# DeltaNet keys and head outputs: scaling by norms moved from GpSimd steps to one VectorE product with broadcast norms

## The chip, the cores and the metric

The kernel runs on one core of one Trainium2 chip. The time is device microseconds (us) of one execution, the median over runs. A profile is one further execution recorded by the hardware profiler. TensorE is called PE in the rows, its weight loads PEld, VectorE is DVE, ScalarE is ACT, GpSimd is POOL and the queue that issues most transfers is SP.

## The reference, cut to what matters

A two-layer encoder trunk over 1024 tokens of width 1024: layer 0 mixes tokens by attention, layer 1 by a bidirectional gated DeltaNet, and each is followed by a convolutional MLP. The change is in the DeltaNet mixer. The lines that it computes are these:

```
def l2norm(x):
    return x * lax.rsqrt(jnp.sum(x * x, axis=-1, keepdims=True) + EPS)
...
    q = jnp.repeat(l2norm(q.reshape(B, S, GDN_QK_HEADS, GDN_DK)) * (GDN_DK ** -0.5), rep, axis=2)
    k = jnp.repeat(l2norm(k.reshape(B, S, GDN_QK_HEADS, GDN_DK)), rep, axis=2)
...
    o = rmsnorm(o_fwd + o_bwd, o_norm) * jax.nn.silu(z ...)
```

There are 8 key heads of 128 numbers and 16 value heads of 128. Each key row of a token and each output row of a token is multiplied by one number, the inverse root of its sum of squares.

## The kernel before, in words

**Layout.** The mixer goes over eight key heads j, each with two value heads. For every j, `gdn_in` projects keys, queries, gates and values (TensorE, `dense`, line 134), runs the width-5 convolution (`conv5`, the VectorE steps on line 448) and prepares what the recurrence needs. `decay` and `inverse` build the inverse triangular matrices of the 128-token chunks, `chain` runs the recurrence over eight chunks in each direction, and `head_out` normalises, gates and stores the two heads.

**Keys.** Behind `kq` in `gdn_in`, the keys lie transposed, so four TensorE transposes (line 533) and a ScalarE copy (473) bring each half of 512 tokens into a tile `h` with tokens on the partitions: four blocks of 128 columns, one block for each 128 tokens. ScalarE sums the squares of each block (484). `rstd` takes the inverse root: a VectorE step (152) and a power on GpSimd (153). Then GpSimd multiplies each of the eight blocks by its column of `r` (line 496, tile `h` out of `h` and `rs`). For each half the result is stored by `put` (a transfer on SP's queue, 468), transposed back by four TensorE transposes (533) and copied to `kT` by ScalarE (499). `kT` feeds the products of line 515.

**Outputs.** In `head_out`, for each half, ScalarE sums squares (756), VectorE corrects them by the query norms (759), `rstd` runs again (152, 153), VectorE multiplies by the query norm (761), and GpSimd scales eight blocks of 128 columns (763, tile `o`). For each value head e, four TensorE transposes (770) read every other block, and VectorE applies the gate (771).

**What sets the order.** The program is written out without loops on the chip. Each instruction gets a priority from a counter that runs in program order; `ahead` lowers the counter for the instructions in it, so that they go before others. `gdn_in`'s key and query block stands in `ahead(2, 1100)`, `decay` and `inverse` in `ahead(4)`, `chain` in `ahead(2)`, and `head_out` has no such mark. When the program is built, a list scheduler lays each engine's instructions into one fixed queue from these priorities, the data they need, and the durations that it assumes. On the chip each queue runs strictly in that order: an instruction that waits holds up everything behind it on its engine. SP's queue, which issues the loads and stores, works the same way.

**Others on the same engines.** GpSimd also scales keys and state in `chain` (705 and 708, tiles `kd` and `sd`), and clears tiles in `inverse` (603, 604). VectorE runs the chain's steps (716, 722, 738, 744), the decay (553, 560, 561, 564), the inverse (608, 609, 624, 628), the weights' low halves (110) and the convolution (448).

Of the kernel before, what the change touches and what calls it, by code (L numbers as in the profile page):

```python
# [13 lines left out]
ALU = mybir.AluOpType  # L14
# [4 lines left out]
P = 128  # L19
# [22 lines left out]
class Trunk:  # L42
# [409 lines left out]
    def gdn_in(self, j, ys, tmp, dp, begun=None):  # L452


        nc = self.nc
        w, cw = self.ap["gdn_in"], self.cw5
        pk = self.dram.tile([NC, P, 5, P], F32, name=f"pk{j}")
        self.pk.append(pk)

        def proj(i):  # L460
            acc = self.big()
            self.dense(acc, self.weights(w[i]), ys)
            return acc

        chunks = lambda t: t.rearrange("p (n c) -> p n c", c=P)

        def put(i, t, ns=slice(0, NC)):
            nc.sync.dma_start(out=pk[ns, :, i].rearrange("n p c -> p n c"), in_=chunks(t))

        def natural(t, i):  # L470
            for h, hs in enumerate(HALVES):
                r = tmp.tile([P, H2], F32, name="h", bufs=2)
                nc.scalar.copy(out=r, in_=self.transposed(t[:, hs]))
                put(i, r, slice(4 * h, 4 * h + 4))

        kq = [self.conv5(acc, cw[:, c], tmp) for acc, c in zip(begun or (proj(8 + j), proj(j)), (8 + j, j))]
        with self.ahead(2, 1100):
            kT, qT = kq
            ss = [dp.tile([P, NC], F32, name="ssn", bufs=2) for _ in range(2)]

            def sums(t, tot):
                for n in range(4):
                    sq = dp.tile([P, P], F32, name="sq", bufs=1)
                    nc.scalar.activation(out=sq, in_=t[:, n * P:(n + 1) * P], func=AF.Square, accum_out=tot[:, n:n + 1])

            kn = []
            for h, hs in enumerate(HALVES):
                t = tmp.tile([P, H2], F32, name="h", bufs=2)
                nc.scalar.copy(out=t, in_=self.transposed(kT[:, hs]))
                sums(t, ss[0][:, 4 * h:4 * h + 4])  # L490
                kn.append(t)
            r = self.rstd(ss[0], 1, dp)
            for h, hs in enumerate(HALVES):
                for n in range(4):
                    t = kn[h][:, n * P:(n + 1) * P]
                    nc.gpsimd.tensor_scalar(out=t, in0=t, scalar1=r[:, 4 * h + n:4 * h + n + 1], scalar2=1.0,
                                            op0=ALU.mult, op1=ALU.mult)
                put(2, kn[h], slice(4 * h, 4 * h + 4))
                nc.scalar.copy(out=kT[:, hs], in_=self.transposed(kn[h]))
            for h, hs in enumerate(HALVES):  # L500
                sums(self.transposed(qT[:, hs]), ss[1][:, 4 * h:4 * h + 4])
            r = self.rstd(ss[1], 1, dp)
            self.rq.append(dp.tile([P, NC, 2], F32, name="rq", bufs=2))
            nc.vector.tensor_scalar(out=self.rq[j], in0=r.unsqueeze(2).broadcast_to([P, NC, 2]),
                                    scalar1=float(P) ** -0.5, scalar2=None, op0=ALU.mult)
            put(0, kT)
            put(1, qT)
            kks, qks = {}, {}
            for i in (1, 0):
                kks[i], qks[i] = (dp.tile([P, H2], F32, name=n, bufs=3) for n in ("kks", "qks"))  # L510
                for rhs, dst in ((kT, kks[i]), (qT, qks[i])):
                    acc = self.bank()
                    for n in range(4):
                        tok = slice((4 * i + n) * P, (4 * i + n + 1) * P)
                        nc.tensor.matmul(acc[:, n * P:(n + 1) * P], lhsT=kT[:, tok], rhs=rhs[:, tok], start=True, stop=True)
                    if rhs is kT:
                        nc.vector.tensor_tensor(out=chunks(dst), in0=chunks(acc), op=ALU.mult,
                                                in1=self.negoff.unsqueeze(1).broadcast_to([P, 4, P]))
                    else:
                        nc.scalar.copy(out=dst, in_=acc)  # L520
        z = lambda e: self.gate_rows(2 * j + e, proj(32 + 2 * j + e), tmp)
        z(0)
        z(1)
        for e in range(2):
            i = 16 + 2 * j + e
            natural(self.conv5(proj(i), cw[:, i], tmp), 3 + e)
        return kks, qks
# [218 lines left out]
    def head_out(self, j, o, dp):  # L746

        nc = self.nc
        od = [self.dram.tile([P, S], F32, name=f"od{2 * j + e}") for e in range(2)]
        for i in (1, 0):  # L750
            hs = HALVES[i]
            ss = dp.tile([P, 8], F32, name="ss", bufs=1)
            of = o[i].rearrange("p n e c -> p (n e) c")
            for m in range(8):
                sq = dp.tile([P, P], F32, name="sq", bufs=1)
                nc.scalar.activation(out=sq, in_=of[:, m], func=AF.Square, accum_out=ss[:, m:m + 1])
            rq = self.rq[j][:, 4 * i:4 * i + 4].rearrange("p n e -> p (n e)")
            for _ in range(2):
                nc.vector.tensor_tensor(out=ss, in0=ss, in1=rq, op=ALU.mult)
            rs = self.rstd(ss, P, dp, tag="ro")  # L760
            nc.vector.tensor_tensor(out=rs, in0=rs, in1=rq, op=ALU.mult)
            for m in range(8):
                nc.gpsimd.tensor_scalar(out=of[:, m], in0=of[:, m], scalar1=rs[:, m:m + 1], scalar2=1.0,
                                        op0=ALU.mult, op1=ALU.mult)
            for e in range(2):
                z = dp.tile([P, H2], F32, name="z", bufs=1)
                nc.sync.dma_start(out=z, in_=self.zd[2 * j + e][:, hs])
                pt = self.bank()
                for n in range(4):
                    nc.tensor.transpose(out=pt[:, n * P:(n + 1) * P], in_=o[i][:, n, e], identity=self.ident)  # L770
                nc.vector.scalar_tensor_tensor(out=z, in0=pt, scalar=self.o_gain, in1=z, op0=ALU.mult, op1=ALU.mult)
                nc.sync.dma_start(out=od[e][:, hs], in_=z)
        self.od += od
# [622 lines left out]
```

## Time and profile before

| What | us |
|---|---|
| median of 3 runs | 3466.25 |
| lowest and highest run | 3457.93, 3467.89 |
| the profiled execution's own time | 3468.96 |
| its span, first to last instruction | 3467.2 |
| DeltaNet stretch looked at, 1368 to 2610 us of the span | 1242 |

The mean granted TensorE clock of the profiled execution is 0.976 of full speed. In the rows further down, "idle before" is the time in which an engine did nothing before an instruction, and the name behind the arrow is the instruction that ended it.

### The profile page before, as it was taken

The numbers are of one execution on the slowest core, as the hardware profiler recorded it, in microseconds if no ns is written. First come the engines' busy times: TensorE is split into PE (matmuls) and PEld (weight loads), VectorE is DVE, ScalarE is ACT, GpSimd is POOL, SyncE is SP. The second block draws the span as 40 slices with busy tenths as digits, with TensorE's granted clock in tenths as the row PEclk, the third lists the DMA queues.
The fourth block names the chain that finished last, engine by engine and source line by source line (L and its number), as shares of the span: only waits on it lengthen the run. The fifth ranks groups of instructions, "written<-read, shape, count | busy, mean of one in ns | idle before, by whom it ended". The sixth has DMA issues, their size and how long they took to land. (4 is left out here: it accounts for less than half of the span.)

```text
span 3467.2 us, 54360 instructions
## 1 busy us (share of the span) xinstructions
PE 3266.1 (94%) x19690; PEld 2627.5 (76%) x19690; DVE 2474.7 (71%) x4203; ACT 1730.5 (50%) x3218; POOL 922.6 (27%) x1111
## 2 busy tenths in 40 slices
PE   7999999899999998899999999999898989999998
PEld 6887878677777776777777777777676867777776
DVE  5325886877776865877768687776853787777695
ACT  4235664544444454466655564555532544544452
POOL 1111220444442001133232223223230144444100
PEclk9999999999999999899999999999999989999999
DMA  4331116333335533233342433324256633332743
GB/s 126 107 113 55 33 33 203 111 110 112 98 101 189 197 116 100 70 112 108 92 145 70 132 109 108 114 82 137 82 190 197 199 103 110 107 99 96 240 132 108
DMA packets 249806, 411.23 MB, mean 119 GB/s; under 512 B 25537, under 2 KB 76097, under 8 KB 249537
## 3 DMA queue, kind: packets, MB, share of 16 engines
q1 hardware_dynamic: 249536, 407.76, 37.7%
q8 instruction: 155, 2.54, 0.3%
q14 instruction: 115, 0.93, 0.1%
HBM read 294.80 MB, written 107.61 MB: 116 GB/s over the span
## 5 line engine op out<-in xcount | busy, mean ns | idle before, releaser
L134 PE MATMUL mm<-base,wh 128*128 128x512 f32 x1248 | 484.0, 415 | 6.5 <-DVE t L448 6.4
L109 ACT CAST wh<-w_raw 128x512 fp32r<-128x512 f32 x275 | 170.1, 619 | 313.9 <-PE mm L134 181.7
L110 DVE TENSOR_TENSOR wl<-w_raw,wh 128x512 fp32r<-128x512 f32 x275 | 195.1, 713 | 150.9 <-ACT wh L109 140.4
L134 PE MATMUL mm<-yh,wh 128*128 128x512 f32 x736 | 286.0, 417 | 5.3 <-ACT t L291 2.7
L134 PE MATMUL mm<-yl,wh 128*128 128x512 f32 x736 | 282.1, 412 | 1.6 <-POOL yl L110 1.0
L153 POOL TENSOR_TENSOR rs<-rs,power 128x8 f32<-128x8 f32 (+2 forms) x38 | 63.4, 1669 | 822.0 <-DVE rs L152 821.7
L134 PE MATMUL mm<-yh,wl 128*128 128x512 f32 x736 | 280.1, 409 | 1.0 <-DVE wl L110 1.0
L134 PEld LDWEIGHTS mm<-base,wh 128*128 128x128 f32 x1248 | 240.4, 193 | 45.8 <-issue 4.2
L134 PE MATMUL mm<-base,wl 128*128 128x512 f32 x624 | 256.9, 412 | 6.2 <-DVE wl L110 6.2
L705 POOL TENSOR_SCALAR kd<-c,yds 128x128 f32<-128x128 f32 x224 | 92.5, 425 | 563.8 <-PE cp L734 373.7
L109 ACT CAST wh<-a 128x512 fp32r<-128x512 f32 x164 | 101.8, 621 | 252.7 <-PE mm L134 115.3
L134 PE MATMUL sp<-base,wh 128*128 128x512 f32 (+1 forms) x672 | 211.5, 373 | 12.4 <-ACT wh L109 12.4
L109 ACT CAST wh<-s 128x512 fp32r<-128x512 f32 x212 | 131.3, 619 | 176.3 <-PE sp L134 98.2
L448 DVE SCALAR_TENSOR_TENSOR t<-mm,gdn_cw,t 128x1023 f32<-128x1023 f32 (+1 forms) x128 | 163.0, 1275 | 8.3 <-ACT t L445 7.4
L134 PEld LDWEIGHTS mm<-yl,wh 128*128 128x128 f32 x736 | 140.9, 192 | 29.0 <-POOL yl L110 2.9
L134 PEld LDWEIGHTS mm<-yh,wh 128*128 128x128 f32 x736 | 140.5, 193 | 29.5 <-ACT t L291 3.6
L134 PEld LDWEIGHTS mm<-yh,wl 128*128 128x128 f32 x736 | 140.9, 192 | 25.5 <-DVE wl L110 1.7
L134 PE MATMUL sp<-base,wl 128*128 128x512 f32 (+1 forms) x432 | 157.6, 365 | 1.4 <-DVE wl L110 0.9
L134 PEld LDWEIGHTS sp<-base,wh 128*128 128x128 f32 x672 | 127.7, 190 | 34.0 <-ACT wh L109 12.8
L110 DVE TENSOR_TENSOR wl<-s,wh 128x512 fp32r<-128x512 f32 x170 | 141.8, 835 | 13.5 <-ACT wh L109 12.9
L982 POOL TENSOR_TENSOR s<-a,a 128x512 f32<-128x512 f32 x80 | 108.4, 1355 | 159.8 <-DVE s L982 106.7
L134 PEld LDWEIGHTS mm<-base,wl 128*128 128x128 f32 x624 | 119.5, 192 | 27.3 <-DVE wl L110 7.1
(522 smaller groups left out, 9417.8 us busy)
## 6 DMA issues: line engine op xcount, KB each, us to landing
a<-in_ffn_up_dram SPq DMA_DIRECT2D x160, 256.0 KB, 3.0
c<-pk SPq DMA_DIRECT2D x128, 320.0 KB, 3.1
w_raw<-in_gdn_in_dram SPq DMA_DIRECT2D x100, 256.0 KB, 2.9
g_t<-t SPq DMA_DIRECT2D x88, 256.0 KB, 2.0
raw<-g_t SPq DMA_DIRECT2D x88, 256.0 KB, 2.7
w_raw<-in_gdn_out_dram SPq DMA_DIRECT2D x68, 256.0 KB, 3.7
g<-t SPq DMA_DIRECT2D x66, 256.0 KB, 2.1
raw<-g SPq DMA_DIRECT2D x66, 256.0 KB, 2.9
```

The costliest lines, as they stand in the source:

```text
L109: self.nc.scalar.copy(out=hi, in_=src)
L110: (engine or self.nc.vector).tensor_tensor(out=lo, in0=src, in1=hi.bitcast(F32), op=ALU.subtract)
L134: self.nc.tensor.matmul(acc if one else acc[:, hs], lhsT=a, rhs=y[:, hs], start=(first and not onto and k + t == 0), stop=(last and k == n ...
L153: nc.gpsimd.tensor_tensor(out=r, in0=v, in1=self.power[:, :w], op=ALU.pow)
L448: nc.vector.scalar_tensor_tensor(out=o, in0=a, scalar=c[:, i:i + 1], in1=o, op0=ALU.mult, op1=ALU.add)
L705: nc.gpsimd.tensor_scalar(out=kd[:, e], in0=kn, scalar1=col(self.yds, e), scalar2=1.0, op0=ALU.mult, op1=ALU.mult)
L982: e.tensor_tensor(out=s[i], in0=x, in1=z, op=op)
```

## The change

The eight GpSimd steps on the keys become two VectorE products, one for each half, each over 128 partitions by 512 columns; the eight GpSimd steps for each half of the outputs become one VectorE product over 1024 columns. The norms enter as a second input that is broadcast along the 128 columns of a block. Nothing else is touched.

```diff
             r = self.rstd(ss[0], 1, dp)
             for h, hs in enumerate(HALVES):
-                for n in range(4):
-                    t = kn[h][:, n * P:(n + 1) * P]
-                    nc.gpsimd.tensor_scalar(out=t, in0=t, scalar1=r[:, 4 * h + n:4 * h + n + 1], scalar2=1.0,
-                                            op0=ALU.mult, op1=ALU.mult)
+                nc.vector.tensor_tensor(out=chunks(kn[h]), in0=chunks(kn[h]), op=ALU.mult,
+                                        in1=r[:, 4 * h:4 * h + 4].unsqueeze(2).broadcast_to([P, 4, P]))
                 put(2, kn[h], slice(4 * h, 4 * h + 4))
                 nc.scalar.copy(out=kT[:, hs], in_=self.transposed(kn[h]))
...
             rs = self.rstd(ss, P, dp, tag="ro")
             nc.vector.tensor_tensor(out=rs, in0=rs, in1=rq, op=ALU.mult)
-            for m in range(8):
-                nc.gpsimd.tensor_scalar(out=of[:, m], in0=of[:, m], scalar1=rs[:, m:m + 1], scalar2=1.0,
-                                        op0=ALU.mult, op1=ALU.mult)
+            nc.vector.tensor_tensor(out=of, in0=of, in1=rs.unsqueeze(2).broadcast_to([P, 8, P]), op=ALU.mult)
             for e in range(2):
```

## Rows read from the trace of the kernel before

**Rows 1.** The page: busy time, share of the span, instructions of each engine.

```profile
PE 3266.1 (94%) x19690; PEld 2627.5 (76%) x19690; DVE 2474.7 (71%) x4203; ACT 1730.5 (50%) x3218; POOL 922.6 (27%) x1111
```

**Rows 2.** Busy time by stretch: the DeltaNet stretch; columns as in the first line.

```profile
core 0: us, PE busy (x) PEld busy (x) DVE busy (x) ACT busy (x) POOL busy (x), PEclk, DMA share, GB/s
1368.00:2610.00 1242.00, 1157.17 (x9881) 911.26 (x9882) 919.66 (x2081) 686.37 (x1525) 337.13 (x685) 0.97 0.38 112
```

**Rows 3.** Groups by shape, GpSimd, that stretch: busy us, mean ns, idle before, releasers.

```profile
L763 POOL TENSOR_SCALAR o<-o,ro 128x128 f32<-128x128 f32 x128 | 60.6, 492 | 9.6 <-DVE ro L761 9.6
...
L153 POOL TENSOR_TENSOR rs<-rs,power 128x8 f32<-128x8 f32 x16 | 26.4, 1647 | 65.6 <-DVE rs L152 65.4
L496 POOL TENSOR_SCALAR h<-h,rs 128x128 f32<-128x128 f32 x64 | 23.1, 381 | 0.8
```

**Rows 4.** Line 496: who waited for it, us in total and times.

```profile
  PEld sp L533: 21.6, 31
...
  DVE st L738: 8.5, 3
```

**Rows 5.** Timeline of one key block: start, us, engine, line, idle before.

```profile
1941.87 1.64 POOL L153 TENSOR_TENSOR rs<-rs,power 128x8 f32<-128x8 f32 x1
...
1943.61 2.80 POOL L496 TENSOR_SCALAR h<-h,rs 128x128 f32<-128x128 f32 x8
1944.04 0.14 PEld L533 LDWEIGHTS sp<-ident,h 128*128 128x128 f32 x1 [2.37 <-POOL h L496]
...
1945.08 0.14 PEld L533 LDWEIGHTS sp<-ident,h 128*128 128x128 f32 x1 [0.21 <-POOL h L496]
...
1946.14 0.46 PEld L533 LDWEIGHTS sp<-ident,h 128*128 128x128 f32 x4
```

**Rows 6.** Line 763: who waited for it, us in total and times.

```profile
  PEld sp L770: 7.7, 8
```

**Rows 7.** Timeline of the last head's two halves of outputs.

```profile
2579.34 0.14 PEld L770 LDWEIGHTS sp<-ident,o 128*128 128x128 f32 x1 [2.52 <-POOL o L763]
...
2600.48 0.17 DVE L761 TENSOR_TENSOR ro<-ro,rq 128x8 f32<-128x8 f32 x1 [1.76 <-POOL ro L153]
2600.82 2.80 POOL L763 TENSOR_SCALAR o<-o,ro 128x128 f32<-128x128 f32 x8 [0.37 <-DVE ro L761]
2601.24 0.14 PEld L770 LDWEIGHTS sp<-ident,o 128*128 128x128 f32 x1 [2.57 <-POOL o L763]
...
2603.32 0.18 PEld L770 LDWEIGHTS sp<-ident,o 128*128 128x128 f32 x1 [0.30 <-POOL o L763]
```

**Rows 8.** Groups by shape, VectorE: products of two tensors.

```profile
L560 DVE TENSOR_TENSOR at<-pr,kks 128x512 f32<-128x512 f32 x64 | 44.4, 694 | 0.9 <-ACT pr L555 0.2
...
L517 DVE TENSOR_TENSOR kks<-sp,negoff 128x512 f32<-128x512 f32 x16 | 11.0, 686 | 6.8 <-PE sp L515 6.8
...
L1039 DVE TENSOR_TENSOR t<-t,t 128x1024 f32<-128x1024 f32 x44 | 53.6, 1219 | 0.0
```

**Rows 9.** Waits of VectorE in the DeltaNet stretch: us in total, times, longest us.

```profile
DVE ro L761 <- POOL ro L153: 22.8, 14, 1.9
...
DVE rq L504 <- POOL rs L153: 9.7, 7, 1.8
```

**Rows 10.** Sixteen 6 us stretches, each from an output power's start: their sum.

```profile
sum 96.00, PE 79.42 PEld 60.82 DVE 61.51 ACT 47.23 POOL 79.11; mean PE 4.96 PEld 3.80 DVE 3.84 ACT 2.95 POOL 4.94
```

**Rows 11.** Timeline behind one output power: VectorE's wait and TensorE's.

```profile
2496.47 0.17 DVE L761 TENSOR_TENSOR ro<-ro,rq 128x8 f32<-128x8 f32 x1 [1.84 <-POOL ro L153]
...
2497.75 0.68 DVE L628 TENSOR_TENSOR x<-ip,lvl 128x512 f16<-128x512 f32 x1
...
2498.48 0.59 PE L595 MATMUL ip<-x,w 128*128 128x32 f16 x16 [2.76 <-DVE x L628]
```

**Rows 12.** 6 us stretches from a key power's start: lowest clock, highest below 1.00.

```profile
1787.82:1793.82 6.00, 4.04 (x16) 2.94 (x16) 2.09 (x6) 1.49 (x4) 4.62 (x10) 0.72 0.35 100
...
2086.53:2092.53 6.00, 3.84 (x17) 2.81 (x16) 2.09 (x6) 1.47 (x4) 4.67 (x10) 0.82 0.34 99
```

## The prediction, made before the change was run

> **What bounds the kernel now.** I read the busy times of the page first. TensorE is busy for 94% of the span, VectorE for 71%, GpSimd for 27% [rows 1], so a microsecond saved on GpSimd is worth something only where TensorE, or something that TensorE soon needs, stood waiting for it. Then I read the busy time of the stretch in which all changed lines run. In its 1242 us TensorE is idle for 1242 - 1157.2 = 84.8 us, and VectorE is busy for 919.7 us, or 74% [rows 2]. Whatever the change can win lies in those 84.8 us, and whatever it costs enters by way of VectorE, the second busiest engine.
>
> The groups by shape give the moved work: 64 steps on keys, 23.1 us, and 128 on outputs, 60.6 us [rows 3]. Next I read who waited for these lines. For the keys TensorE's transposes did, 21.6 us in all, and VectorE's state update three times, 8.5 us [rows 4]. For the outputs it was 7.7 us [rows 6], and the timeline shows where: two groups at the last head open with waits of 2.52 and 2.57 us, and the pauses behind them make up the rest [rows 7]. The other fourteen halves of outputs let nobody wait, so there a quicker scaling is worth nothing.
>
> The timeline of one key block shows that the scaling is the smaller part of the wait. The inverse root on GpSimd takes 1.64 us, and the first transpose starts 0.43 us after the first scaling step; of its 2.37 us of waiting most belongs to the root, which stays [rows 5].
>
> **The change part by part.** *Keys, TensorE's side.* Eight steps take 2.80 us, 0.35 each, and transposes start with them: the first 0.43 us and the fourth 1.47 us behind the first step's start [rows 5]. So the hand-over takes 0.43 - 0.35 = 0.08 us. The new product is 128 by 512 with a broadcast second input. The nearest row is a product of that size out of SBUF, also with a broadcast input, 694 ns; one out of PSUM takes 686 [rows 8]. Neither repeats one number along the innermost columns, as the norms do. I take 0.694 us; the lower end is 0.686, the upper end the four GpSimd steps that it replaces, 4 x 0.35 = 1.40. The first transpose then starts at 0.694 + 0.08 = 0.77, and four of them back to back take 0.46 us [rows 5], so the fourth starts at 0.77 + 0.35 = 1.12, or 0.35 us sooner. For eight heads: **-2.8 us**. The second half was ready in time before, and is ready sooner now, 2 x 0.694 = 1.39 against 2.80 us.
>
> This price can be set against a rule. The Trainium skill (GPSIMD Engine Reference, Engine selection) calls elementwise work with one tensor input roughly line rate on GpSimd, which speaks against moving it. By that rule the four steps would cost about what one product does, this term would be zero and the whole sum below -0.6 us; the trace's 1.40 against 0.694 us disagrees, because the steps come in small pieces, and I go by the rows.
>
> *Outputs, TensorE's side.* The fourth transpose of the group starts 2.67 us after the end of the last VectorE step (2600.65 to 2603.32) [rows 7]. A product of 1024 columns takes 1.219 us [rows 8]. With hand-over and three transposes that gives 1.22 + 0.08 + 0.35 = 1.65, or 1.0 us sooner, twice: **-2.0 us**. Bounds: nothing, or all 7.7 us.
>
> *GpSimd's queue.* The chain's scalings of keys and state (lines 705 and 708) no longer stand behind 2.80 us of steps. Of the 8.5 us that the state update waited [rows 4], part belongs to TensorE's delay in the same places, so I take about half, **-4 us**, between 0 and -8.5.
>
> *VectorE's work.* 16 x 0.694 + 16 x 1.219 = 30.6 us are added. The stretch loses 84.8 us of TensorE to 919.7 us of VectorE work [rows 2], 0.092 us for each: **+2.8 us**. The lower end is 0, since TensorE has projections of its own to run meanwhile. For the upper end I look at the sixteen stretches behind an output power. TensorE is idle there for 96.00 - 79.42 = 16.6 us [rows 10]; less the 7.7 that waited for GpSimd, 8.9 us stand against 22.8 us in which VectorE was held by the power [rows 9], a share of 0.39. That makes +11.9 us.
>
> *A new wait on VectorE.* The key product needs the root. For outputs and queries VectorE already sits out the root, 14 and 7 times [rows 9], so its next step is put right behind the power, and I expect the key product there too. It stands at the head of VectorE's queue for up to 1.65 us [rows 3], 13.2 us for eight heads; behind it stand the chain's steps, the convolution and the inverse, and TensorE waits for those. TensorE is held by the same root at that moment, so I take half of the share above, 0.39 x 13.2 / 2 = **+2.6 us**, with ends 0 and 13.2.
>
> *Store of the keys.* It waits for VectorE instead of GpSimd on SP's queue, with the chunk loads and the decay's row loads behind it. For the first half that is 0.77 against 1.47 us after the power if VectorE is free. I cost it at nothing; if VectorE comes late, the loads do too, which the slower rival holds.
>
> **The sum.** -2.8 - 2.0 - 4 + 2.8 + 2.6 = -3.4 us against the profiled execution's 3468.96 us, so 3465.6. That execution was 2.7 us above the median of 3466.25, so I predict **3463 us** for the median: no change, since 0.3%, or 10.4 us, is about what a measurement of this kernel can tell.
>
> **The rivals.** *Slower: the root holds VectorE's queue.* In one place before, VectorE waits 1.84 us for an output root, a step of the inverse behind it comes late, and TensorE stands for 2.76 us [rows 11]. With the change a key block has 1.65 us of waiting and 1.39 us of products there, eight times, 24.3 us. If 0.6 of that reaches TensorE, and 0.39 of the output products' 19.5 us, the result is 14.6 + 7.6 - 4.8 = +17 us, or 3483. It becomes measurably slower from a share of 0.31 on, since 24.3 x 0.31 + 7.6 - 4.8 = 10.3. For it: the wait shown. Against it: in the key block shown, TensorE waits for the root itself.
>
> *Faster: the clock holds and the chain is freed.* Behind five of the eight key powers TensorE's granted clock lies between 0.72 and 0.82 over 6 us, so part of the time is at 1.2 instead of 2.4 GHz [rows 12]; TensorE was idle, then ran scattered transposes ahead of it. Over 30 us, 0.18 to 0.28 are missing, 5.4 to 8.4 us. If denser transposes keep the clock up (-7) and all 8.5 us of state waits go, the sum is -2.8 - 2.0 - 8.5 - 7 + 2.8 = -17.5, or 3449. Against it: the first transpose starts 0.34 us later than before, so the idle time ahead of it grows.
>
> *The product costs what it replaces.* At 1.40 us for 512 columns and 2.80 for 1024, the fourth transposes come 0.35 us later for keys and 0.56 for outputs, +2.8 and +1.1, and the added work doubles to 67 us, +6.2. With -4 and +2.6 that is +8.7, or 3475. No row speaks for it.
>
> Under all of them lies a new instruction order: the scheduler sees other engines and durations, and every queue behind the first changed block may come out differently. Neither sign is favoured; it widens the range.
>
> **How the numbers follow.** I give the forecast 0.44, the slower rival 0.25, the faster 0.29 and the costly product 0.02. The range runs from the faster rival's side, 3446, to somewhat beyond the slower one's, 3486; its ends lie near the bounds of the terms (-2.8 - 7.7 - 8.5 = -19, and 11.9 + 13.2 - 2.8 = +22). The cases within 10.4 us are the forecast and the costly product, but order alone can carry the forecast out on either side, so I keep 0.44 for no change, 0.30 for faster and 0.26 for slower.
>
> **What the changed profile would show.** Products near 694 and 1219 ns. TensorE's waits at line 533 near 2.7 us at the first transpose and none between the four. VectorE waiting for the root eight more times, for 1 to 1.8 us. GpSimd 84 us less busy, VectorE some 31 us more. Idle time of TensorE in the stretch near 82 us. I would be wrong if the waits of TensorE for VectorE steps of chain and inverse grew by more than some 15 us together, or if the clock behind the key blocks no longer fell.

## The result, and the profile after

The median went from 3464.48 us (6 runs, measured again beside the change) to **3438.07 us** (6 runs, 3436.47 to 3443.46). The ratio is 0.9932, with a 95% interval from 0.9920 to 0.9944: faster by 26 us by the medians and by 24 by the ratio. The forecast was 3463 with a range from 3446 to 3486, so the result lies 8 us below the low end and 25 us below the number. The profiled execution of the changed kernel took 3439.26 us with a span of 3437.5.

The page of the changed kernel, busy time by engine, answers to [rows 1]:

```profile
PE 3247.3 (94%) x19690; PEld 2620.0 (76%) x19690; DVE 2495.2 (73%) x4235; ACT 1741.5 (51%) x3224; POOL 842.4 (25%) x919
```

GpSimd lost 80 us and VectorE gained 20.5 us net. TensorE is *busy* 19 us less with the same number of instructions, and that is the line to stop at: waiting that goes away shortens idle time, not busy time.

The groups by shape of the changed kernel for the changed lines and the root (DeltaNet stretch), as in [rows 3] and [rows 8]:

```profile
L760 DVE TENSOR_TENSOR o<-o,ro 128x1024 f32<-128x1024 f32 x16 | 19.5, 1218 | 0.2
...
L494 DVE TENSOR_TENSOR h<-h,rs 128x512 f32<-128x512 f32 x16 | 10.7, 686 | 11.7 <-POOL rs L153 11.7
...
L759 DVE TENSOR_TENSOR ro<-ro,rq 128x8 f32<-128x8 f32 x16 | 2.9, 178 | 17.6 <-POOL ro L153 17.6
```

The products cost 686 and 1218 ns against forecasts of 694 and 1219. The new wait of VectorE for the key root is there: 11.7 us in front of line 494.

To see where the time went, compare the stretch in which the changed lines run, from the first key root to the end of layer 1's mixer, by busy times. Kernel before, then the changed kernel; the columns are the stretch, its length, then busy us of PE, PEld, DVE, ACT and POOL, the granted clock, DMA share and GB/s:

```profile
1366.87:2663.80 1296.93, 1208.41 (x10111) 953.31 (x10109) 940.74 (x2115) 699.91 (x1547) 337.94 (x685) 0.97 0.39 116
```

```profile
1368.60:2636.10 1267.50, 1188.03 (x10111) 945.90 (x10109) 961.92 (x2147) 710.31 (x1554) 256.92 (x493) 0.98 0.37 118
```

The stretch shrank by 29.4 us, all of the span's 29.7. TensorE's idle time in it fell from 1296.93 - 1208.41 = 88.5 to 79.5 us, that is by 9.0. The other 20.4 us are busy time of the same 10111 instructions. Mean granted clock over the span, kernel before and changed kernel:

```profile
core 0: 3467.2 us, clock 0.976
```

```profile
core 0: 3437.5 us, clock 0.981
```

Missing clock is 3467.2 x 0.024 = 83.2 us before and 3437.5 x 0.019 = 65.3 us after: 17.9 us, give or take 2.5 for the rounding. So about one third of this profile's gain is waiting, and of the two thirds that are busy time the larger part goes with TensorE running at 2.4 instead of 1.2 GHz for more of the time. The profiled execution of the kernel before had somewhat more half-clock time than most. Every timed run lists its clock: over the 79 runs of that kernel beside the experiments the mean is 0.978, or 76 us missing (single runs 0.974 to 0.982), over the six of the changed kernel 0.982, or 62 us. So 14 us is the better figure for the clock.

**The waiting.** TensorE's own waits in that stretch (us in total, times, longest), kernel before:

```profile
PE sp L533 <- POOL h L496: 14.0, 8, 2.0
PE ip L595 <- DVE w L609: 9.5, 17, 2.0
PE ip L595 <- DVE w L624: 8.1, 6, 1.9
PE cp L712 <- DVE st L738: 7.0, 10, 2.1
PE ip L595 <- DVE x L628: 6.0, 3, 2.8
PE sp L770 <- POOL o L763: 5.3, 5, 2.1
PE cp L728 <- DVE r L716: 5.2, 7, 1.2
...
PE sp L515 <- DVE kks L517: 2.2, 4, 0.9
```

The same view of the changed kernel, where most line numbers are 2 lower:

```profile
PE ip L593 <- DVE w L607: 11.7, 20, 1.7
PE ip L593 <- DVE w L622: 10.0, 9, 1.5
PE sp L531 <- DVE h L494: 9.2, 7, 1.8
PE sp L513 <- DVE kks L515: 6.7, 7, 1.6
PE mm L134 <- ACT base L109: 5.9, 1, 5.9
PE cp L726 <- DVE r L714: 4.6, 7, 1.2
PE ip L593 <- DVE x L626: 3.3, 5, 1.0
...
PE sp L766 <- DVE o L760: 3.2, 2, 1.9
...
PE cp L710 <- DVE st L736: 1.8, 3, 0.8
```

Waits for scaled keys fell by 4.8 us, for scaled outputs by 2.1, for the state update by 5.2: 12.1 together. A later step of the key path on VectorE, the masked product of keys (`kks`), is now waited for 4.5 us longer. The waits for the inverse's three steps and for the residual `r` changed by +2.2, +1.9, -2.7 and -0.6, +0.8 together. So 12.1 us of waits went and 5.3 came: -6.8 of the -9.0 us of idle time. The remaining -2.2 us are a balance of waits at unchanged lines, among them a single new one of 5.9 us, of a projection for a ScalarE cast (`base`, line 109).

**A key block.** Timeline of the changed kernel at the fourth head (start, us, engine, line, idle before), as in [rows 5]:

```profile
1790.52 1.65 POOL L153 TENSOR_TENSOR rs<-rs,power 128x8 f32<-128x8 f32 x1
...
1792.20 0.69 DVE L494 TENSOR_TENSOR h<-h,rs 128x512 f32<-128x512 f32 x1 [1.97 <-POOL rs L153]
1792.81 0.60 DVE L714 SCALAR_TENSOR_TENSOR r<-cp,negc,c 128x128 f32<-128x128 f32 x2
1792.95 0.20 PEld L531 LDWEIGHTS sp<-ident,h 128*128 128x128 f32 x2 [2.19 <-DVE h L494]
...
1793.33 0.68 DVE L494 TENSOR_TENSOR h<-h,rs 128x512 f32<-128x512 f32 x1
```

VectorE stands 1.97 us in front of the product, and the chain's step of line 714 queues behind it. The first transpose comes 0.75 us behind the product's start (0.77 forecast), and the pauses of 0.21 us between the transposes are gone. Now the 8 us from each key root's start. Kernel before, three of its eight blocks, and the sum of all eight:

```profile
1367.19:1375.19 8.00, 6.38 (x27) 4.87 (x26) 1.55 (x4) 4.23 (x8) 4.45 (x9) 0.79 0.26 79
1500.78:1508.78 8.00, 6.18 (x37) 4.64 (x36) 4.96 (x12) 2.45 (x5) 6.24 (x14) 1.00 0.45 124
...
1787.82:1795.82 8.00, 6.04 (x28) 4.64 (x28) 2.94 (x8) 2.60 (x6) 4.62 (x10) 0.79 0.49 140
...
sum 64.00, PE 49.52 PEld 38.03 DVE 25.47 ACT 25.73 POOL 41.96; mean PE 6.19 PEld 4.75 DVE 3.18 ACT 3.22 POOL 5.24
```

The same three blocks and the sum in the changed kernel:

```profile
1368.95:1376.95 8.00, 6.54 (x38) 5.30 (x37) 2.50 (x7) 6.11 (x10) 1.64 (x1) 1.00 0.38 112
1499.76:1507.76 8.00, 8.00 (x48) 6.60 (x48) 7.56 (x17) 4.25 (x7) 5.66 (x9) 1.00 0.61 188
...
1790.52:1798.52 8.00, 6.24 (x39) 4.90 (x39) 4.32 (x12) 3.39 (x9) 2.38 (x4) 1.00 0.44 138
...
sum 64.00, PE 54.77 PEld 45.23 DVE 38.49 ACT 33.13 POOL 26.15; mean PE 6.85 PEld 5.65 DVE 4.81 ACT 4.14 POOL 3.27
```

TensorE's idle time in these eight windows fell from 64 - 49.52 = 14.5 to 9.2 us. Five of the eight blocks before had a granted clock of 0.79, which is 8 x 0.21 = 1.7 us missing each, 8.4 in all; after, none is below 1.00. The second block shows something that the forecast had no term for: TensorE has no idle time at all there, because the new instruction order put projection products in front of the transposes. Key blocks and last head together explain 5.3 + 8.4 + 2.1 = 15.8 us of the 29.4, if each us of missing clock is taken as a us of time. At the last head, two stretches fell below full clock before and one after, some 1.7 us more. The rest comes from places that hold no changed line.

### The profile page after: what moved, and what is told of

It reads as the page before. It is cut to its first block, busy times and chain, and to the rows that moved or that the text cites. A ratio compares the mean times of both kernels' runs of the same rounds, so it can differ in the third digit from the quotient of the medians.

```text
span 3437.5 us, 54135 instructions
## 1 busy us (share of the span) xinstructions
PE 3247.3 (94%) x19690; PEld 2620.0 (76%) x19690; DVE 2495.2 (73%) x4235; ACT 1741.5 (51%) x3224; POOL 842.4 (25%) x919
```

## The experiments

Each kernel was timed in five rounds beside the kernel before on the same chip; ratios are to that.

### One part alone

`e1_keys` keeps the GpSimd steps on the outputs, `e2_outs` those on the keys:

```diff
 e1_keys, against the kernel before
-                    nc.gpsimd.tensor_scalar(out=t, in0=t, scalar1=r[:, 4 * h + n:4 * h + n + 1], scalar2=1.0,
+                nc.vector.tensor_tensor(out=chunks(kn[h]), in0=chunks(kn[h]), op=ALU.mult,
...
 e2_outs, against the kernel before
-                nc.gpsimd.tensor_scalar(out=of[:, m], in0=of[:, m], scalar1=rs[:, m:m + 1], scalar2=1.0,
+            nc.vector.tensor_tensor(out=of, in0=of, in1=rs.unsqueeze(2).broadcast_to([P, 8, P]), op=ALU.mult)
```

> Only the keys go to VectorE; the outputs stay in eight GpSimd steps. Waiting theory (the gain comes where TensorE stood for the key scaling, and from its clock behind that): the eight key blocks lose some 5 us of idle TensorE time and some 8 us of half-clock time, as in the changed kernel, so the time is 11 to 17 us below the kernel before, ratio 0.995 to 0.997. Order theory (the new instruction order of the whole stretch gains, not the waits): no relation to the key blocks; the ratio can be anywhere, also above 1, and the key-only and output-only gains need not add up to 26 us.

Measured: 3448.37 us, 0.9937 [0.9919, 0.9955], or -20 us beside 3468.44, somewhat more than the 11 to 17 of the waiting theory.

> Only the outputs go to VectorE; the keys stay in GpSimd steps. Waiting theory: TensorE waited for output steps at the last head alone, so 2 to 6 us at most are won and the five half-clock stretches behind the key blocks stay; ratio 0.998 to 1.000. Order theory: may be anywhere. GpSimd theory (freeing GpSimd for the chain's scalings is what counts, and the outputs are 61 of its 84 us): two thirds of the gain, 17 us, ratio 0.995.

Measured: 3451.36 us, 0.9947 [0.9933, 0.9961], or -17 us. At the key blocks the two separate cleanly: 8 us windows have 6.9 us of idle time and no block below full clock in `e1_keys`, 16.2 us and five blocks at 0.79 in `e2_outs`. But `e2_outs` gained 17 us where only 2 us of waiting for outputs were to be had on TensorE, so the waiting theory fails here, and the two parts sum to 37 us where the whole gave 26. The GpSimd theory had named 17 us, but its mechanism is not there in that size: the wait for the state update fell from 7.0 to 4.4 us, and the one for the residual `r` rose from 5.2 to 11.7. Something else moves with the parts.

### The instruction order alone

The instruction streams say what. Compared place by place in the two traces (buffers of one name counted as the same), some 7,100 of 19,690 TensorE instructions differ, from the first key block on. The scheduler writes one list from the durations that it assumes, and another engine or duration can change the list behind it. To get other orders without other work, the key block's priority mark is changed:

```diff
-        with self.ahead(2, 1100):
+        with self.ahead(2, 500):      # or 2000, or 1300
```

> The kernel before with the priority offset of the key and query block at 500 instead of 1100: no work is moved, only the order of the instructions differs. Waiting theory: within 8 us of the kernel before, ratio 0.998 to 1.002. Order theory: order alone moves the time by 10 us or more, ratio below 0.997 or above 1.003.

> The kernel before with that offset at 2000: a third order of the same instructions. Waiting theory: ratio 0.998 to 1.002. Order theory: below 0.997 or above 1.003, and not the same as with 500.

> The changed kernel with the priority offset at 500: the same work in another order. Waiting theory with order as a second cause: the key blocks keep their clock (none or one half-clock stretch of eight) and the time stays 12 to 25 us below the order-only kernel of the same offset (3458), so 3433 to 3446, ratio 0.990 to 0.9945. Order theory: the changed kernel's 0.993 was a lucky order; this one falls to 0.996 to 1.000.

> The same with the offset at 2000. Waiting theory with order as a second cause: 0.990 to 0.9945, key blocks with their clock. Order theory: 0.996 to 1.000.

> The kernel before, with the key block's priority mark at 1300 in place of 1100, so that only the instruction order differs: a fourth order. If order alone is worth 10 us and more either way, this lies anywhere between 3440 and 3480 us, and outside 3463 to 3468. If the shipped order of the kernel before was simply a bad one and nearly every other order is better, it lies near 3458, as the other two orders did.

> The changed kernel in the same fourth setting. Theory of the moved work: TensorE's idle time and half-clock stretches at the eight key blocks go, 5 us and 8.5 us, and 2.4 us at the last head, so this is 10 to 17 us below the kernel before at 1300. Theory of the order: the pair differs by something unrelated to that, as the three pairs so far do (-26, -12 and +16 us), and it may have either sign; a positive difference here would make the mean of the four pairs about nothing.

Measured, ratio to the kernel before and median in us. The last column is the changed kernel with an early root, told of further down:

| mark | before | changed | changed, early root |
|---|---|---|---|
| 1100 | 1 | 0.9932, 3438.07 | 0.9856, 3418.11 |
| 500 | 0.9969, 3458.41 | 0.9933, 3442.66 | 0.9906, 3434.96 |
| 2000 | 0.9961, 3457.88 | 1.0008, 3468.71 | 0.9909, 3437.44 |
| 1300 | 1.0036, 3476.38 | 0.9960, 3453.87 | 0.9932, 3439.73 |
| mean of ratios | 0.9992 | 0.9958 | 0.9901 |

The same work in another order is worth 19 us for the kernel before (3457.88 to 3476.38) and 31 us for the changed one. In pairs with the same mark the change gives -0.68, -0.36, +0.47 and -0.76%; in us of 3467 that is -24, -12, +16 and -26, with a mean of -12 and a standard error of 10. So a good part of the measured 26 us may belong to the order that the scheduler happened to lay, and four orders don't pin the rest. Of the expectations, `e3`, `e4` and `e13` bear out the order theory, though 500 and 2000 come out alike. `e5` lies in the waiting theory's range, but with two half-clock blocks where none or one was expected; `e6` lies beyond both ranges. `e14` gains more against `e13` than the 10 to 17 us named.

What holds in every pair is the picture at the key blocks. From the 8 us windows, worked out as above:

| mark | idle before, after | blocks below full clock, missing us before, after |
|---|---|---|
| 1100 | 14.5, 9.2 | 5 (8.4), 0 |
| 500 | 16.2, 10.5 | 5 (8.4), 2 (4.9) |
| 2000 | 15.4, 10.7 | 4 (6.7), 1 (1.7) |
| 1300 | 15.3, 7.9 | 7 (11.8), 0 |
| mean | 15.4, 9.6 | 5.2 (8.8), 0.8 (1.6) |

That is -5.8 us of idle time and -7.2 of clock; with the -2.1 us at the last head (mark 1100) it makes 15 us that go with the moved work in each of these orders, and agree with the mean of -12. Each row is one profiled execution of each kernel, and the count of blocks varies from one execution to another: `e11` further down has the order of the kernel before until behind the last key block, and the same idle time (14.4 us), but only two blocks below full clock. The sums over four orders, 21 against 3 of 32 blocks, are the safer reading.

Where order takes it back shows at mark 2000. TensorE's waits there, first in the kernel before (`e4`), then in the changed one (`e6`):

```profile
PE cp L728 <- DVE r L716: 14.7, 16, 1.6
...
PE ip L595 <- DVE w L624: 5.8, 6, 1.9
...
PE ip L674 <- DVE w L683: 2.8, 5, 1.0
```

```profile
PE cp L726 <- DVE r L714: 15.5, 18, 1.7
PE ip L593 <- DVE w L622: 14.5, 10, 2.0
...
PE ip L672 <- DVE w L681: 9.2, 11, 1.8
```

The chain's residual costs some 15 us in both kernels at this mark, against about 5 at 1100, so it is no part of the pair's loss. The inverse's two steps `w` are: 14.5 against 5.8 us and 9.2 against 2.8. The scaled keys are better, 10.7 us against 14.9. The loss shown is in the inverse, in VectorE's queue, at lines that did not change. (The profiled execution of `e4` was its fastest, 3447.12 us against a median of 3457.88.)

### A product, or only another engine?

`e7_dve_key_steps` keeps eight small steps for the keys, on VectorE; `e8_gpsimd_key_product` makes the product on GpSimd. Outputs as in the change.

```diff
 e7_dve_key_steps, against the kernel before
-                    nc.gpsimd.tensor_scalar(out=t, in0=t, scalar1=r[:, 4 * h + n:4 * h + n + 1], scalar2=1.0,
+                    nc.vector.tensor_scalar(out=t, in0=t, scalar1=r[:, 4 * h + n:4 * h + n + 1], scalar2=1.0,
 e8_gpsimd_key_product, against the changed kernel
-                nc.vector.tensor_tensor(out=chunks(kn[h]), in0=chunks(kn[h]), op=ALU.mult,
+                nc.gpsimd.tensor_tensor(out=chunks(kn[h]), in0=chunks(kn[h]), op=ALU.mult,
```

> The changed kernel with the keys scaled on VectorE in eight steps of 128 columns instead of two products: same engine, small pieces. If one product and back-to-back transposes matter, the fourth transpose comes later, and some of the half-clock stretches behind the key blocks return: 3 to 10 us slower than the changed kernel. If only leaving GpSimd matters, the same within 3 us.

> The changed kernel with the keys scaled in one GpSimd product for each half (outputs stay on VectorE): one product, but on the slow engine, some 1.4 us each. If back-to-back transposes are what holds the clock, it holds here too although they come 0.7 us later, and the time is within 6 us of the changed kernel. If the length of TensorE's wait is what counts, the half-clock stretches come back in four or more of eight key blocks and the time goes to that of the output-only kernel, 3451, or above.

Measured: `e7` 3451.04 us, 0.9960 [0.9947, 0.9972]; `e8` 3452.91 us, 0.9964 [0.9952, 0.9976]. The groups by shape, `e7` and then `e8`:

```profile
L496 DVE TENSOR_SCALAR h<-h,rs 128x128 f32<-128x128 f32 x64 | 14.2, 286 | 5.9 <-POOL rs L153 5.8
```

```profile
L494 POOL TENSOR_TENSOR h<-h,rs 128x512 f32<-128x512 f32 x16 | 16.8, 1068 | 0.6
```

Four steps on VectorE cost 4 x 0.286 = 1.14 us where the product costs 0.686; one product on GpSimd costs 1.068 where four steps take 1.40 [rows 5]. Both are between the two kernels in price. At the key blocks `e7` has 5.5 us of idle time and one block below full clock, `e8` 17.7 us and three. The same split runs through all kernels with a single root for both halves: 5.5 to 10.7 us of idle time in the six that scale keys on VectorE, 14.4 to 17.7 in the seven that do it on GpSimd (`e9` and `e10`, with a doubled key root, left aside). So the idle time at the key blocks goes with the engine, and the single product is the smaller part. Whether that is the shorter scaling or the place that the scheduler then gives to projection products is not shown; `e7` has three blocks without any idle time. Against the whole time `e7` and `e8` cannot be told apart, and both differ from the changed kernel by as much as orders do.

### A wait with the order held

A second power behind the first changes nothing else: the TensorE, VectorE and ScalarE streams of `e9` and the kernel before are the same instruction by instruction, and in `e10` and `e11` some 30 to 40 TensorE instructions differ from the kernels that they start from. So these price a wait with almost no new order.

```diff
-            r = self.rstd(ss[0], 1, dp)
+            r = self.rstd(ss[0], 1, dp, times=2)      # e9, e10: the power runs twice
-            rs = self.rstd(ss, P, dp, tag="ro")
+            rs = self.rstd(ss, P, dp, tag="ro", times=2)      # e11
```

> The kernel before, with the key root on GpSimd computed twice into the same tile: 1.65 us more ahead of each key scaling, eight times, 13.2 us in all, with every other engine's order as before, instruction for instruction. If the key blocks' wait is on the path that sets the end: +13 us or somewhat more (three more key blocks can lose their clock, 1.7 us each), ratio 1.003 to 1.006. If TensorE makes the wait good from other work: within 4 us, ratio 0.999 to 1.001.

> The changed kernel with the key root twice: 13.2 us more, and nearly the same order (36 of 21095 TensorE rows differ). If the length of TensorE's wait is what takes the clock: +13 us plus up to 13 us of half-clock time, six to eight key blocks with a stretch, 3451 to 3464, ratio 0.996 to 1.000. If back-to-back transposes hold the clock whatever the wait: +13 us and no stretch, 3449 to 3453. If the wait is made good: within 4 us of 3438.

> The kernel before with the output root computed twice: VectorE, which waits for it, is held 16 times for 1.65 us more, 26.4 us, with nearly the order of before (25 of 21056 TensorE rows). The share of it that reaches the end prices work and waits put on VectorE: the sum in the prediction took 0.39 for a wait and 0.09 for work. At 0.39: +10 us, ratio 1.003. At 1: +26 us, ratio 1.0076. At 0.09: +2 us, ratio 1.0007.

Measured: `e9` 3484.51 us against 3467.29, +17 us (1.0050 [1.0037, 1.0062]), for 8 x 1.65 = 13.2 us of root. `e10` 3462.64 (0.9986 [0.9976, 0.9995]), for the same 13.2 us +19 us over the changed kernel by the ratios and +24 by the medians (3438.07, timed in another session). `e11` 3494.60, +27 us (1.0075 [1.0063, 1.0088]), for 16 x 1.65 = 26.4 us. TensorE's longest waits in `e9`, then `e10`:

```profile
PE sp L533 <- POOL h L496: 27.6, 8, 3.7
PE ip L595 <- DVE w L609: 9.5, 17, 1.9
```

```profile
PE sp L531 <- DVE h L494: 18.4, 8, 3.3
```

TensorE pays the root in full in `e9`: 14.0 becomes 27.6 us. `e11` says more: the output root is not waited for by TensorE, only by VectorE's line 761, and still about each us of it reaches the end. And doubling the power left the order as it was; that the scheduler would cover the root if it knew its length is not tested.

The clock at the key blocks answers the question that `e10` was built for. One block of `e9` and one of `e10`, 12 us from the start of the first power:

```profile
1795.35:1807.35 12.00, 8.32 (x37) 6.71 (x37) 3.21 (x10) 3.00 (x8) 6.80 (x13) 0.72 0.46 136
```

```profile
1799.39:1811.39 12.00, 8.79 (x40) 7.33 (x38) 4.32 (x12) 3.35 (x9) 4.01 (x5) 0.72 0.32 92
```

With the longer wait, all eight blocks of `e9` fall below full clock (five before), and five of `e10` (none in the changed kernel). In `e10`'s block at 2103.77 us the first four transposes run back to back, 0.65 us together, and the clock falls behind them all the same (0.86 over the 12 us), so the theory that such transposes hold the clock whatever the wait is out. The wait's length counts, and the clock lost with it can be why more than 13.2 us reached the end.

### The root earlier

In the changed kernel the root of all eight blocks waits for both halves. With a root for each half, right behind its squares, it can run beside the second half's transposes:

```diff
-            kn = []
+            kn, r = [], []
...
+                r.append(self.rstd(ss[0][:, 4 * h:4 * h + 4], 1, dp))
-            r = self.rstd(ss[0], 1, dp)
...
-                                        in1=r[:, 4 * h:4 * h + 4].unsqueeze(2).broadcast_to([P, 4, P]))
+                                        in1=r[h].unsqueeze(2).broadcast_to([P, 4, P]))
```

> The changed kernel with a root of its own for each half of the keys, started as soon as that half's squares are summed: the first half's root is shorter (four columns instead of eight) and starts earlier, so TensorE's wait at the key blocks, 9 us idle in eight stretches of 8 us, should shrink to 2 to 6. Waiting theory: 3 to 8 us faster than the changed kernel, 3430 to 3435, ratio 0.990 to 0.992, unless the new order takes it back. Order theory: 3428 to 3465, with no relation to the key blocks.

> The changed kernel with a root of its own for each half of the keys, right behind that half's squares, in the fourth setting. If the root's wait is what is left at the key blocks, this is 10 to 25 us below the changed kernel at 1300, as the early root was in the shipped setting (-20 us). If that gain was a lucky order, the difference is within 10 us or positive.

> The changed kernel with the early root, key mark at 500. So far the early root gained 20 us in the shipped setting and 14 us at 1300. If the gain is the root's wait gone from the key blocks, this is 10 to 20 us below the changed kernel at 500 (3443), so 3423 to 3433 us. If the order decides, the difference may be anything within 15 us of nothing.

> The changed kernel with the early root, key mark at 2000, where the changed kernel lost its gain (3469 us). If the early root is worth its 10 to 20 us in any order, this is 3449 to 3459 us. If the loss at 2000 came from the place of the key block in the order (too early or too late for the chain's loads and steps), which the early root does not mend, it stays within 8 us of 3469.

> The kernel before, scalings still in single GpSimd steps, with only the early root for each half. If the root is the costly part of the key block and the GpSimd steps are not, this is 15 to 25 us below the kernel before, near 3445, and the product adds little to it. If the two act together (the steps between root and transposes keep TensorE stuttering and the clock at half), it is at most 8 us below the kernel before, and the half-clock stretches at the key blocks stay (5 of 8 blocks).

Measured: `e12` **3418.11 us**, 0.9856 [0.9843, 0.9870], 49 us below the kernel before and the best of all. The other three orders are in the table above (`e15` 0.9932 [0.9915, 0.9949], `e17` 0.9906 [0.9889, 0.9924], `e18` 0.9909 [0.9891, 0.9927]). Against the changed kernel with the same mark the early root gives -0.76, -0.27, -0.99 and -0.28%: faster in all four, 20 us in the mean with a standard error of 6. `e17` gained 8 us where 10 were the least expected, `e15` lies at the low end of its 10 to 25 us, and `e18` mended the loss at 2000 altogether, where the theory of a bad place had it near 3469. `e12` itself went far beyond the 3 to 8 us of the waiting theory.

Timeline of `e12` at the fourth head: the root is shorter (four columns, 1.02 against 1.65 us), and VectorE works all through it, on a convolution step and the inverse's `w`:

```profile
1786.99 1.27 DVE L448 SCALAR_TENSOR_TENSOR t<-mm,gdn_cw,t 128x1022 f32<-128x1022 f32 x1
...
1787.16 1.02 POOL L153 TENSOR_TENSOR rs<-rs,power 128x4 f32<-128x4 f32 x1 [4.87 <-DVE rs L152]
...
1788.29 0.69 DVE L681 SCALAR_TENSOR_TENSOR w<-w,ip 128x512 f32<-128x512 f16 x1
...
1788.89 0.68 DVE L494 TENSOR_TENSOR h<-h,rs 128x512 f32<-128x512 f32 x1
```

TensorE's wait for scaled keys in `e12`, against 9.2 us in the changed kernel:

```profile
PE sp L531 <- DVE h L494: 4.8, 6, 1.1
```

`e16`, the early root with the GpSimd steps, reached 3454.62 us, 0.9973 [0.9963, 0.9983]: -13 us, between the two expectations. Two key blocks stay below full clock, idle time in the windows is 10.7 us. So neither theory is right alone: root and place of the scaling each seem to count. This is one order of each kernel, though, and order alone moves the time by as much.

## Why the prediction was wrong

The local terms of the forecast's sum lie within about 2 us of the rows each, not all of them for the reason given. The forecast failed in two steps that it did name, but kept out of the sum: the clock and the order. Its own sign of being wrong came true: the clock behind the key blocks no longer fell.

- **Product prices, hand-over.** Right: 686 and 1218 ns, and 0.75 us to the first transpose. That the products might cost what they replace is out. The reason given, small pieces, holds in the main: four steps take 1.14 us on VectorE too. The rule set against the price there (the Trainium skill, GPSIMD Engine Reference, Engine selection) also says of elementwise work with two inputs that GpSimd is about twice as slow as VectorE; for this product the runs show 1068 against 686 ns, 1.56 times.
- **Keys, TensorE's side, -2.8.** TensorE's waits fell by 4.8 us. The surplus is no shorter hand-over but projection products that the new order put into two of the eight blocks.
- **Outputs, -2.0.** -2.1 by the waits. Right.
- **GpSimd's queue, -4.** -5.2 at the state update. Right in size.
- **VectorE's work and new wait, +2.8 and +2.6.** The wait came, 7 times and 11.7 us. What TensorE waits longer for is `kks`, +4.5, and about +0.8 at the inverse and the residual, 5.3 against 5.4. The size agrees by luck: the chain and the inverse, which the forecast named, hardly paid, and that `kks` is late because of the added work is not shown.
- **The clock: the step that failed.** The forecast put it into the faster rival and took nothing of it into the sum, on the ground that the first transpose would come later and lengthen the idle time. The first transpose did come later behind the root, 0.75 us against 0.43. But the idle time at the key blocks shrank, from 14.5 to 9.2 us, two thirds of it in the two blocks with projection products, and the half-clock blocks went from 5 to 0 of 8; in four orders from 21 to 3 of 32. This alone is 8 us in the profiled pair, and over the whole span 18, or 14 in the mean of all runs. The rival's own -7 for it was right; its chance was low, since the rows of before already showed the price five times in eight.
- **The order: "neither sign is favoured; it widens the range".** True, but the range was not widened by it: its ends were the bounds of the local terms. Measured, order alone is worth 19 us (before) and 31 us (changed) from best to worst. A range of the local sum with the clock, 3466 - 3 - 8 = 3455, and some 20 us to each side for the order would have held the result.
- **The slower rival** took VectorE's wait at a share of 0.6 and the 0.39 of [rows 9, 10]. With the order held, that share is about 1 or more (13.2 us gave 17 and 19 to 24, 26.4 gave 27). Why the rival did not come true is not shown: TensorE was held by the same root before, and the order was laid anew around the product. At mark 2000 the changed kernel is 16 us above the kernel before by the ratios. There TensorE waits longer for the inverse's `w`, but whether VectorE's wait for the root does that is not shown.

**What stays open.** How the 26 us divide exactly. The local part, 15 us in the mean of four orders, is shown by windows; the whole, -12 with a standard error of 10, agrees but would agree with 0 nearly as well. What a us of missing clock is worth is open too: over the 79 runs of the kernel before, an estimate from clock and time of each run gives 0.6 us of time. And why the clock falls at some blocks and not at others: a longer wait brings it down (`e9`, `e10`), but `e8` had more idle time at the key blocks (17.7 us) than the kernel before and fewer blocks below full clock (3), and `e11`, in the same order, had 2.

## What to carry to other kernels

Where a list scheduler lays the queues, a small edit is two edits, the local one and a new order. Time the old and the new kernel in a few orders (a priority mark moved in both is enough) before a gain of 1% is put down to the local one, and look at the windows for what holds in each order. A row with a clock below full at the place of the edit belongs into the sum as a price, and not only among the rivals. And when a stall has two parts in a row, here a root of 1.65 us and a scaling of 0.77, start with the longer: moving the root forward gave 20 us more in the mean of four orders, and 13 us alone (`e16`).

## What the runs showed of the hardware

Half-clock time followed idle time of TensorE and outlasted it. Kernel before, busy times of the 6 us around [rows 11] and of the 20.5 us behind them:

```profile
2490.50:2496.50 6.00, 3.65 (x46) 2.76 (x45) 4.09 (x13) 2.90 (x4) 1.65 (x2) 1.00 0.68 186
2496.50:2517.00 20.50, 13.87 (x195) 10.59 (x195) 18.49 (x38) 7.79 (x13) 2.80 (x8) 0.50 0.37 124
```

TensorE was idle for 2.35 of 6 us, and then had 20.5 us at 0.50. That is 10 us of missing clock, which need not be 10 us of lost time: TensorE was busy for 13.87 us of the 20.5 and VectorE for 18.49, so VectorE was the fuller engine there, and what the half clock cost in that stretch is not shown. The Trainium skill (TensorE: Matmul & The Clock Gate, Part 1) describes two levels, 2.4 and 1.2 GHz, with the lower as the state that idling falls back to; the granted clock of 0.50 here agrees with the levels.

The power on GpSimd is priced by more than columns: 1.65 us for eight columns, 1.02 for four. Splitting the root in two costs 2 x 1.02 - 1.65 = 0.4 us of GpSimd for each head.
